# Diagonal prefix sums: the last block's fold, row sums and last 64 places placed differently over the engines

## The chip, the cores and the metric

The kernel runs on one core of one Trainium2 chip. The metric is the device time in microseconds of one execution. PE is the tensor engine (TensorE), DVE the vector engine (VectorE), ACT the scalar engine (ScalarE), POOL GpSimd, and SP the sync engine, which here only issues writes and one early load.

## The reference

```python
B, H, W = 4, 4224, 4224          # x: float32
ps = np.cumsum(np.cumsum(x, axis=1), axis=2)
diag = np.diagonal(ps, axis1=1, axis2=2)
return np.cumsum(diag, axis=1)   # (4, 4224)
```

Place i of the result is the sum, over all k up to i, of the sum of the k+1 by k+1 corner of x. An element in row r and column c therefore counts in place i with the weight i - max(r, c) + 1, where that is positive.

## The kernel before

Only elements on and below the diagonal band are needed row by row, and those right of it column by column, but together they are the whole of x: 285 MB are read. All loads but one are issued by POOL in float32 and land in SBUF as bf16. For each of the four batches the rows are taken in strips of 768 (tile `strip`, six rows on each of 128 partitions), and a last strip of 384. Three strip buffers let the loads run ahead of the work.

`add_up` handles a strip. TensorE adds the columns right of the strip's diagonal square into `d` (PSUM, 11 groups of 384 places), by matmuls whose stationary operand is one column of ones placed by `sel`. VectorE cuts the part above the diagonal out of the square (`mu`) and takes it out of the strip. ScalarE (`act_sum`, an ACTIVATE with an accumulator) and VectorE (`row_sums`) share the sums along the rows. At the end of a batch the row sums go into `d` too, and two scans along the places turn `d` into the results: `whole_sums` for batches 0 to 2, `last_sums` for batch 3.

The last batch ends in a stretch of its own, since nothing comes after it that could hide its work. Its last 384 rows (from `T0` on) are split. Their first 256 are part a (`part_a`, two halves of 128 rows), of which the columns of `head` were loaded at the very start. The last 128 rows are part b (`part_b`): four blocks of R = 32 rows, each spread over all 128 partitions as 32 rows by 4 pieces of 1024 columns, one load a block, with the last block cut into 768 and 256 columns. The diagonal square of part b is `diag_b`; it is loaded and summed (`dtot`) after strip 1 of the last batch.

The last 384 places are then gathered on one partition in three PSUM rows: `fin_a` (the first 256), `fin_b` (the last 128) and `fin_e` (what block 3 adds to the last 32). `weigh_a` and `weigh_b` are matmuls with a column of row sums as the stationary operand and a weight matrix streaming: `weights[p, i]` is i - p + 1 where positive, and `weights4` is the same for part b's blocks, where four partitions share a row. In order, as the code lists it: the fold of part a by `ident_h` into `fold_a`; block 0 by eight matmuls into `fold`, copied to `by` by ScalarE; `dtot`; the first row of `last_sums`; VectorE's `row_sums` of `fold_a` and their sum with the head's (`arows`); `by`; the four matmuls with `arows`; blocks 1 and 2, each summed half by ScalarE and half by VectorE (`pair_sum`, into `bsum`) and weighed into `fin_b`; block 3 in three pieces (`esum`), weighed into `fin_e`; and the sum of `fin_e` with the last 32 of `fin_b`, as `ye`.

The order is written by hand: the schedule is manual, so each engine runs its instructions in program order, and a wait holds up all that stands behind it on that engine. SP issues, in this order: the load of `head`; `yl`'s first 256 places; `whole_sums`; `last_sums`; `yl`'s next 96; `ye`, the last 32. POOL issues the loads. The lines that matter in the profile are L225 and L232 (all matmuls, by `matmul` and `matmul_on`), L267 (`act_sum`), L272 (`row_sums`), L282 (`pair_sum`), L498 (the scans), L533 (the copy to `by`), L540 (`arows`), L554 and L573 (`yl`), L579 (`ye`), and the writes L555, L558, L561, L574 and L580.

Of the kernel before, what the change touches and what calls it, by code (L numbers as in the profile page):

```python
# [8 lines left out]
FP32 = mybir.dt.float32  # L9
BF16 = mybir.dt.bfloat16  # L10
I32 = mybir.dt.int32
AX = mybir.AxisListType
# [5 lines left out]
def kernel(  # L18
# [14 lines left out]
    nc = tc.nc  # L33

    B, H, W = x.shape
    N = H
    P = 128
    F = 3
    F2 = 2 * F
    GW = P * F  # L40
# [3 lines left out]
    T0 = LG * GW  # L44
# [4 lines left out]
    consts = ctx.enter_context(tc.tile_pool(name="consts", bufs=1))  # L49
# [4 lines left out]
    last = ctx.enter_context(tc.tile_pool(name="last", bufs=1))  # L54
# [41 lines left out]
    hs = last.tile([P, 3], FP32, name="hs")  # L96
# [25 lines left out]
    for i in range(1, NBUF):  # L122
# [51 lines left out]
    def between_groups(name, turned):  # L174
# [35 lines left out]


    R = P // 4
    steps = consts.tile([P, P], I32, name="steps")
    nc.gpsimd.iota(steps, pattern=[[4, P]], base=7, channel_multiplier=-1)
    nc.vector.tensor_single_scalar(
        out=steps, in_=steps, scalar=2, op=ALU.arith_shift_right
    )
    weights4 = consts.tile([P, P], FP32, name="weights4")
    nc.vector.tensor_scalar_max(out=weights4, in0=steps, scalar1=0.0)

    ident_h = consts.tile([P, P], BF16, name="ident_h")
    nc.vector.tensor_copy(out=ident_h, in_=ident)
# [1 line left out]
    def matmul(o, lhsT, rhs, start=False):  # L224
        nc.tensor.matmul(  # L225
            o, lhsT=lhsT, rhs=rhs, start=start, stop=False, skip_group_check=True
        )

    def matmul_on(o, lhsT, rhs):

        te = nc.tensor
        te.add_instruction(  # L232
            mybir.InstMatmult(
                start_tensor_calc=False,
                stop_tensor_calc=False,
                tile_position=(0, 0),
                tile_size=(P, P if lhsT.shape[-1] > 64 else 32),
                bass_skip_group_check=True,
                ldweights=False,
                name=nc.get_next_instruction_name(),  # L240
                engine=te.engine,
                ins=[
                    te.lower_ap(rhs, opt=False),
                    te.lower_ap(lhsT, opt=False, for_matmul_weights=True),
                ],
                outs=[te.lower_ap(o)],
            )
        )

    weights4_h = consts.tile([P, P], BF16, name="weights4_h")  # L250
    nc.vector.tensor_copy(out=weights4_h, in_=weights4)
    ones_col = consts.tile([P, 1], FP32, name="ones_col")
    nc.vector.memset(ones_col, 1.0)

# [9 lines left out]
    def act_sum(acc, src):  # L264
        w = src.shape[-1]
        dump = dumpool.tile([P, 2176], BF16, name="dump")
        nc.scalar.activation(  # L267
            out=dump[:, :w], in_=src, func=ACT.Copy, accum_out=acc
        )

    def row_sums(acc, src):
        nc.vector.reduce_sum(out=acc, in_=src, axis=AX.X)  # L272
# [3 lines left out]
    def pair_sum(acc, src):  # L276

        w = src.shape[-1] // 2
        if not pairs:
            pairs.append(last.tile([P, 288], FP32, name="pair"))  # L280
        pair = pairs[0]
        nc.vector.scalar_tensor_tensor(  # L282
            out=pair[:, :w],
            in0=src[:, :w],
            scalar=1.0,
            in1=src[:, w:],
            op0=ALU.mult,
            op1=ALU.add,
            accum_out=acc,
        )  # L290
# [23 lines left out]
        nc.vector.memset(rows3[i], 0.0)  # L314


    asum = last.tile([P, 2, 2], FP32, name="asum")
    dtot = last.tile([P, 1], FP32, name="dtot")
    hu = last.tile([P, 3], FP32, name="hu")
    hmu = last.tile([P, 3, GW], BF16, name="hmu")  # L320
    for h in range(2):
        w = GW - h * P
        masked(hmu[:, h, :w], head[:, h, HC - w : HC], um1[:, :w], hu[:, h : h + 1])
    nc.vector.tensor_sub(out=asum[:, :, 0], in0=hs[:, 0:2], in1=hu[:, 0:2])

    whole_sums = last.tile([NG, LB, GW], FP32, name="whole_sums")
    last_sums = last.tile([NG, GW], FP32, name="last_sums")

    for b in range(B):
        whole = b < LB  # L330
# [8 lines left out]

        def row_of(j):  # L340
            return (j + t0) % NG

        def columns(j, lo, hi, rhs, same=False):
# [53 lines left out]
        for s in range(ns):  # L397
            strip = prefetched.pop(0) if prefetched else None
            if strip is None:
                strip = strip_tile()  # L400
                load_rows(strip, b, s * F2 * P)
            add_up(
                strip, F2, s * F2 * P, acc6[:, s], um6, by_rows=whole and s > 0
            )
            if not whole and s == 0:
                diag_b = last.tile([P, P], BF16, name="diag_b")
                nc.gpsimd.dma_start(out=diag_b, in_=x[b, TB:N, TB:N])
            if not whole and s == 1:
                row_sums(hs[:, 2:3], diag_b)
                masked(hmu[:, 2, :P], diag_b, um1[:, :P], hu[:, 2:3])  # L410
                nc.vector.tensor_sub(out=dtot, in0=hs[:, 2:3], in1=hu[:, 2:3])
                for h in range(3):
                    columns(LG, h * P, GW, hmu[:, h, : GW - h * P], h > 0)
        a6 = acc6[:, :ns]
        sum_up(a6)
        for h in range(2):
# [90 lines left out]
            continue  # L507


        M0 = 2 * P  # L510
        E0 = GW - R
        fin_a = psum_s.tile([1, M0], FP32, name="fin_a")
        fin_b = psum_s.tile([1, P], FP32, name="fin_b")
        fin_e = psum_s.tile([1, R], FP32, name="fin_e")
        yl = last.tile([1, GW], FP32, name="yl")
        ye = last.tile([1, R], FP32, name="ye")

        def weigh_a(rows, w, start=False):

            matmul(fin_a, rows, w[..., :M0], start=start)  # L520

        def weigh_b(rows, w, r0=0, start=False):

            matmul(fin_b[:, r0:], rows, w[..., : P - r0], start=start)


        c0, c1 = acuts[1]
        fold_in(fold_a, part_a, c0, c1, 256)
        by_ps = psum_s.tile([P, P], FP32, name="fold")
        for c in range(0, CB, P):  # L530
            matmul(by_ps, part_b[:, 0, c : c + P], weights4_h, start=c == 0)
        by = last.tile([P, P], FP32, name="by")
        nc.scalar.copy(out=by, in_=by_ps)  # L533
        weigh_b(dtot, weights, start=True)
        weigh_b(ones_col[0:1], last_sums[0:1, M0:])


        row_sums(asum[:, :, 1], fold_a)
        arows = last.tile([P, 2], FP32, name="arows")
        nc.vector.tensor_add(out=arows, in0=asum[:, :, 0], in1=asum[:, :, 1])  # L540
        weigh_b(ones_col, by)
        weigh_a(arows[:, 0:1], weights, start=True)
        matmul(fin_a[:, P:], arows[:, 1:2], weights[:, :P])
        weigh_b(arows[:, 0:1], weights[:, M0:])
        weigh_b(arows[:, 1:2], weights[:, P:])


        bsum = last.tile([P, 2, 2], FP32, name="bsum")
        esum = last.tile([P, 3], FP32, name="esum")
        act_sum(bsum[:, 0, 0:1], part_b[:, 1, :512])  # L550
        pair_sum(bsum[:, 0, 1:2], part_b[:, 1, 512:])
        for i in (1, 0):
            weigh_b(bsum[:, 0, i : i + 1], weights4, R)
        nc.vector.tensor_add(out=yl[:, :M0], in0=fin_a, in1=last_sums[0:1, :M0])  # L554
        nc.sync.dma_start(  # L555
            out=out[b, T0 : T0 + M0].unsqueeze(0), in_=yl[:, :M0]
        )
        nc.sync.dma_start(  # L558
            out=out[:LB, :].rearrange("b (g i) -> g b i", i=GW), in_=whole_sums
        )  # L560
# [2 lines left out]
        )  # L563
        act_sum(bsum[:, 1, 0:1], part_b[:, 2, :448])
        pair_sum(bsum[:, 1, 1:2], part_b[:, 2, 448:])
        for i in (1, 0):
            weigh_b(bsum[:, 1, i : i + 1], weights4, 2 * R)


        act_sum(esum[:, 0:1], part_b[:, 3, :320])  # L570
        pair_sum(esum[:, 1:2], part_b[:, 3, 320:bcut])
        pair_sum(esum[:, 2:3], part_b[:, 3, bcut:])
        nc.scalar.copy(out=yl[:, M0:], in_=fin_b)  # L573
        nc.sync.dma_start(  # L574
            out=out[b, T0 + M0 : T0 + E0].unsqueeze(0), in_=yl[:, M0:E0]
        )
        for k in (1, 0, 2):
            matmul(fin_e, esum[:, k : k + 1], weights4[:, :R], start=k == 1)
        nc.vector.tensor_add(out=ye, in0=fin_e, in1=yl[:, E0:])  # L579
        nc.sync.dma_start(out=out[b, T0 + E0 : N].unsqueeze(0), in_=ye)  # L580


# [28 lines left out]
```

## Time and profile before

| | |
|---|---|
| median of 10 runs | 667.34 us (667.16 to 667.73) |
| the profiled execution's own time | 667.34 us |
| its span, first to last instruction | 665.6 us |
| busy: PE / DVE / ACT / POOL | 205.9 / 380.9 / 136.1 / 31.7 us |
| DMA | 143.23 MB moved as written to SBUF and HBM, 215 GB/s mean; HBM read 285.47 MB |
| last load issued by POOL | 634.03 us |
| batch 2's last scan (`whole_sums` complete) | ends 521.33 us |
| batch 3's last scan (`last_sums` complete) | ends 659.78 us |
| SP's issue of `whole_sums` / `last_sums` / `ye` | 662.23 / 662.59 / 663.69 us |

All stamps count from the start of the span. A line of the timeline gives the start, the duration, the engine, the line of the code, the operation, and the tiles it writes and reads; in brackets stands the idle time of the engine before it and what ended that. A matmul in float32 is run as two passes, so "x4" of such matmuls are two. PEld is the load of a matmul's stationary operand. A line of the DMA view gives a queue (q0 POOL's, q1 SP's), its packets, its megabytes, and its share of the 16 DMA engines' time in the stretch.

### The profile page before, as it was taken

Reading aid. Unit: us, or ns where it says so; the run is one execution under the profiler, and the core shown is the slowest. Engines: PE = TensorE matmul, PEld = TensorE weight load, DVE = VectorE, ACT = ScalarE, POOL = GpSimd, SP = SyncE. Lnnn points to the kernel's source line nnn. Section 1 sums busy time; section 2 is a strip of 40 time slices with the busy share of each in tenths; the row PEclk is TensorE's granted clock in tenths of the full one; section 3 lists DMA queues with packets and bytes.
Section 4 is the critical chain, followed back from the end, with each engine's and each line's share of the span. In section 5 each row is a group of like instructions: output and inputs, shape, how many; then the busy total and the mean of one; then the engine's idle time right before and its main releaser. Section 6 shows DMA issues by size and latency. Waiting matters only on the chain.

```text
span 665.6 us, 2498 instructions
## 1 busy us (share of the span) xinstructions
PE 205.9 (31%) x948; PEld 93.8 (14%) x948; DVE 380.9 (57%) x176; ACT 136.1 (20%) x219; POOL 31.7 (5%) x60
## 2 busy tenths in 40 slices
PE   0071522302117143140311723404021354350428
PEld 0030211100003021010100311201000131120103
DVE  4161828476946173756794526456589433352866
ACT  0001120406300103040630020304063002030434
POOL 4300000000000000000000000000000000001000
PEclk9995857656559585665655857657565595775758
DMA  9999999999999999999999999999999999999998
GB/s 203 219 219 219 219 219 219 213 210 212 219 219 219 218 220 219 218 213 215 212 219 220 217 216 219 219 218 219 209 218 216 220 215 218 219 218 218 215 206 163
DMA packets 7666, 143.23 MB, mean 215 GB/s; under 512 B 698, under 2 KB 998, under 8 KB 2150
## 3 DMA queue, kind: packets, MB, share of 16 engines
q0 software_dynamic: 7312, 142.47, 100.0%
q1 hardware_dynamic: 342, 0.61, 0.4%
q8 instruction: 7, 0.11, 0.1%
q14 instruction: 5, 0.04, 0.0%
HBM read 285.47 MB, written 0.07 MB: 429 GB/s over the span
## 4 chain that ended last, share of the span: by engine, by line
DVE 50%; another core or an unknown queue 32%; DMA 14%; POOL 1%; issue 1%; PE 1%; DVEq 0%; POOLq 0%
DVE acc L272 26%; DMA strip<-in_x_dram 14%; DVE rowed L272 7%; DVE mu L367 7%; DVE strip L368 7%; PE d L225 1%; POOL um L107 1%; DVE um L106 1%; DMA head<-in_x_dram 1%; DVE c L498 0%; DVE whole_sums L498 0%; POOL strip L463 0%; DVE pu L272 0%; DVE whole_sums L293 0%
## 5 line engine op out<-in xcount | busy, mean ns | idle before, releaser
L267 ACT ACTIVATE dump<-strip 128x416 bf16<-128x416 bf16 (+6 forms) x108 | 124.4, 1152 | 520.3 <-DMA strip<-in_x_dram 517.6
L367 DVE TENSOR_TENSOR mu<-strip,um 128x4608 bf16<-128x4608 bf16 (+1 forms) x24 | 52.4, 2184 | 255.2 <-DMA strip<-in_x_dram 255.1
L272 DVE TENSOR_REDUCE acc<-strip 128x6 f32<-128x4608 bf16 (+6 forms) x23 | 195.9, 8519 | 0.4
L232 PEld LDWEIGHTS <-sel 128*11 128x11 bf16 x643 | 66.4, 103 | 477.2 <-issue 447.7
L225 PE MATMUL d<-strip,sel 128*11 128x384 bf16 x90 | 37.0, 411 | 281.9 <-DMA strip<-in_x_dram 281.9
L232 PE MATMUL d<-strip,sel 128*11 128x384 bf16 x441 | 116.3, 407 | 13.8 <-DMA strip<-in_x_dram 13.8
L368 DVE TENSOR_TENSOR strip<-strip,mu 128x4608 bf16<-128x4608 bf16 (+1 forms) x24 | 52.4, 2183 | 1.0
L225 PE MATMUL d<-mu,sel 128*11 128x384 bf16 x43 | 16.3, 379 | 108.4 <-DVE mu L367 108.4
L272 DVE TENSOR_REDUCE rowed<-strip 128x384 f32<-128x2304 bf16 x12 | 48.9, 4078 | 0.0
L232 PE MATMUL d<-mu,sel 128*11 128x384 bf16 x200 | 46.2, 365 | 0.0
L76 POOL DMA_DIRECT2D strip<-in_x_dram x23 | 15.6, 680 | 535.6 <-DVE acc L272 293.6
L267 ACT ACTIVATION_READ_ACCUMULATOR dump<-strip 128x1 f32 x108 | 20.1, 186 | 0.0
L225 PE MATMUL d<-rowed,sel_f 128*11 128x384 f32 x24 | 11.8, 580 | 21.0 <-DVE rowed L272 21.0
L225 PEld LDWEIGHTS <-sel 128*11 128x11 bf16 x134 | 13.6, 102 | 24.4 <-issue 12.5
L225 PE MATMUL d<-ident,rows 128*11 128x128 f32 x24 | 5.2, 378 | 16.8 <-DVE rows L428 16.8
L272 DVE TENSOR_REDUCE pu<-d 11x1 f32<-11x384 f32 x4 | 2.2, 545 | 6.2 <-PE d L225 6.2
L107 POOL TENSOR_SCALAR_AFFINE_SELECT um<-um 128x4608 bf16<-128x4608 bf16 (+1 forms) x2 | 5.2, 2621 | 8.6 <-DVE um L106 8.5
L106 DVE MEMSET um<- 128x4608 bf16 (+1 forms) x2 | 4.9, 2458 | 1.1 <-issue 1.1
L225 PE MATMUL d<-halves,rows 128*11 128x64 f32 x48 | 5.3, 288 | 0.0
L225 PEld LDWEIGHTS d<-ident,rows 128*11 128x11 f32 x24 | 2.5, 117 | 18.9 <-DVE rows L428 11.7
L225 PEld LDWEIGHTS d<-rowed,sel_f 128*11 128x11 f32 x24 | 1.4, 92 | 25.5 <-DVE rowed L272 25.2
L225 PEld LDWEIGHTS d<-halves,rows 128*11 128x11 f32 x48 | 4.8, 128 | 1.3 <-issue 1.1
(106 smaller groups left out, 62.0 us busy)
## 6 DMA issues: line engine op xcount, KB each, us to landing
strip<-in_x_dram POOLq DMA_DIRECT2D x18, 6336.0 KB, 72.7
strip<-in_x_dram POOLq DMA_DIRECT2D x7, 3168.0 KB, 55.8
strip<-in_x_dram POOLq DMA_DIRECT2D x1, 1080.0 KB, 49.9
strip<-in_x_dram POOLq DMA_DIRECT2D x1, 768.0 KB, 52.8
strip<-in_x_dram POOLq DMA_DIRECT2D x3, 256.0 KB, 54.1
head<-in_x_dram SPq DMA_DIRECT2D x1, 528.0 KB, 3.7
strip<-in_x_dram POOLq DMA_DIRECT2D x1, 192.0 KB, 43.2
strip<-in_x_dram POOLq DMA_DIRECT2D x1, 64.0 KB, 28.6
```

The lines of the kernel that those rows point to most:

```text
L76: nc.gpsimd.dma_start(out=o, in_=x[b, r0 : r0 + f * P, :].rearrange("(p f) w -> p f w", f=f))
L106: nc.vector.memset(um, 1.0)
L107: nc.gpsimd.affine_select(out=um, in_=um, compare_op=ALU.is_gt, fill=0.0, base=0, pattern=[[-1, f], [1, f * P]], channel_multiplier=-f,)
L225: nc.tensor.matmul(o, lhsT=lhsT, rhs=rhs, start=start, stop=False, skip_group_check=True)
L232: te.add_instruction(mybir.InstMatmult(start_tensor_calc=False, stop_tensor_calc=False, tile_position=(0, 0), tile_size=(P, P if lhsT.shap ...
L267: nc.scalar.activation(out=dump[:, :w], in_=src, func=ACT.Copy, accum_out=acc)
L272: nc.vector.reduce_sum(out=acc, in_=src, axis=AX.X)
L367: nc.vector.tensor_mul(out=mu, in0=block, in1=um)
L368: nc.vector.tensor_sub(out=block, in0=block, in1=mu)
```

## The change

The change touches the last stretch and what it needs. ScalarE sums `fold_a` by two ACTIVATEs into `asum`, in place of VectorE's `row_sums`; the head's row sums (`ahead`) are no longer added to them, but weighed by matmuls of their own, together with `dtot`, right after strip 1 of the last batch. `fin_a`, `fin_b` and `fin_e` are allocated at the start of that batch for it.

The last 64 places (S = 64, 32 before) go to 64 partitions: `fin_e` becomes 64 by 129. Its last column takes the last 64 of `yl`, turned onto partitions by a one-row matmul, and block 2's weighed sums; its other 128 columns take block 3, which is no longer summed first: TensorE streams it in eight pieces of 128 columns, with `weights4_hw`, the bf16 weights widened by 32 columns, as the stationary operand. VectorE sums the 129 columns into `ye`, 64 partitions of one value, and `ye` is written from there. The copy of `fin_b` into `yl` moves from ScalarE to VectorE and ahead of block 2's weighing; `yl` is written once, as 320 places, after `whole_sums` and `last_sums`.

```diff
-    steps = consts.tile([P, P], I32, name="steps")
-    nc.gpsimd.iota(steps, pattern=[[4, P]], base=7, channel_multiplier=-1)
+    steps = consts.tile([P, R + P], I32, name="steps")
+    nc.gpsimd.iota(steps, pattern=[[4, R + P]], base=7 - 4 * R, channel_multiplier=-1)
...
-    weights4 = consts.tile([P, P], FP32, name="weights4")
-    nc.vector.tensor_scalar_max(out=weights4, in0=steps, scalar1=0.0)
+    weights4_w = consts.tile([P, R + P], FP32, name="weights4_w")
+    nc.vector.tensor_scalar_max(out=weights4_w, in0=steps, scalar1=0.0)
+    weights4 = weights4_w[:, R:]
...
-    weights4_h = consts.tile([P, P], BF16, name="weights4_h")
-    nc.vector.tensor_copy(out=weights4_h, in_=weights4)
+    weights4_hw = consts.tile([P, R + P], BF16, name="weights4_hw")
+    nc.vector.tensor_copy(out=weights4_hw, in_=weights4_w)
+    weights4_h = weights4_hw[:, R:]
...
-    nc.vector.tensor_sub(out=asum[:, :, 0], in0=hs[:, 0:2], in1=hu[:, 0:2])
+    nc.vector.tensor_sub(out=ahead, in0=hs[:, 0:2], in1=hu[:, 0:2])
...
+    M0 = 2 * P
+    S = 2 * R
+    E0 = GW - S
...
+        if not whole:
+            fin_a = psum_s.tile([1, M0], FP32, name="fin_a")
+            fin_b = psum_s.tile([1, P], FP32, name="fin_b")
+            fin_e = psum_s.tile([S, P + 1], FP32, name="fin_e")
...
+        def weigh_rows(rows, start=False):
+
+            matmul(fin_a, rows[:, 0:1], weights[:, :M0], start=start)
+            matmul(fin_a[:, P:], rows[:, 1:2], weights[:, :P])
+            weigh_b(rows[:, 0:1], weights[:, M0:])
+            weigh_b(rows[:, 1:2], weights[:, P:])
...
                     columns(LG, h * P, GW, hmu[:, h, : GW - h * P], h > 0)
+                weigh_b(dtot, weights, start=True)
+                weigh_rows(ahead, start=True)
...
+        for h in range(2):
+            act_sum(asum[:, h : h + 1], fold_a[:, h])
         by = last.tile([P, P], FP32, name="by")
         nc.scalar.copy(out=by, in_=by_ps)
-        weigh_b(dtot, weights, start=True)
         weigh_b(ones_col[0:1], last_sums[0:1, M0:])
-
-
-        row_sums(asum[:, :, 1], fold_a)
-        arows = last.tile([P, 2], FP32, name="arows")
-        nc.vector.tensor_add(out=arows, in0=asum[:, :, 0], in1=asum[:, :, 1])
+        weigh_rows(asum)
         weigh_b(ones_col, by)
-        weigh_a(arows[:, 0:1], weights, start=True)
-        matmul(fin_a[:, P:], arows[:, 1:2], weights[:, :P])
-        weigh_b(arows[:, 0:1], weights[:, M0:])
-        weigh_b(arows[:, 1:2], weights[:, P:])
...
         nc.vector.tensor_add(out=yl[:, :M0], in0=fin_a, in1=last_sums[0:1, :M0])
         nc.sync.dma_start(
-            out=out[b, T0 : T0 + M0].unsqueeze(0), in_=yl[:, :M0]
-        )
-        nc.sync.dma_start(
             out=out[:LB, :].rearrange("b (g i) -> g b i", i=GW), in_=whole_sums
         )
...
         pair_sum(bsum[:, 1, 1:2], part_b[:, 2, 448:])
+        nc.vector.tensor_copy(out=yl[:, M0:], in_=fin_b)
+        nc.sync.dma_start(
+            out=out[b, T0 : T0 + E0].unsqueeze(0), in_=yl[:, :E0]
+        )
+
+
+        matmul(fin_e[:, P:], yl[:, E0:], ones_col[0:1], start=True)
         for i in (1, 0):
-            weigh_b(bsum[:, 1, i : i + 1], weights4, 2 * R)
-
-
-        act_sum(esum[:, 0:1], part_b[:, 3, :320])
-        pair_sum(esum[:, 1:2], part_b[:, 3, 320:bcut])
-        pair_sum(esum[:, 2:3], part_b[:, 3, bcut:])
-        nc.scalar.copy(out=yl[:, M0:], in_=fin_b)
-        nc.sync.dma_start(
-            out=out[b, T0 + M0 : T0 + E0].unsqueeze(0), in_=yl[:, M0:E0]
-        )
-        for k in (1, 0, 2):
-            matmul(fin_e, esum[:, k : k + 1], weights4[:, :R], start=k == 1)
-        nc.vector.tensor_add(out=ye, in0=fin_e, in1=yl[:, E0:])
-        nc.sync.dma_start(out=out[b, T0 + E0 : N].unsqueeze(0), in_=ye)
+            matmul(fin_e[:, P:], weights4[:, :S], bsum[:, 1, i : i + 1])
+        for c in range(0, CB, P):
+            piece = part_b[:, 3, c : c + P]
+            if c == 0:
+                matmul(fin_e[:, :P], weights4_hw[:, :S], piece, start=True)
+            else:
+                matmul_on(fin_e[:, :P], weights4_hw[:, :S], piece)
+        nc.vector.reduce_sum(out=ye, in_=fin_e, axis=AX.X)
+        nc.sync.dma_start(out=out[b, T0 + E0 : N].unsqueeze(1), in_=ye)
```

`matmul_on` is `matmul` without a new start of its accumulation; it takes a tile size of 64 columns besides 32 and 128. On SP, `whole_sums` is now the first issue after the load of `head`, and waits for VectorE's scan alone.

More of the change, by code (lines that the diff above doesn't have):

```diff
@@ L236, in matmul_on @@
                 tile_position=(0, 0),
-                tile_size=(P, P if lhsT.shape[-1] > 64 else 32),
+                tile_size=(P, P if lhsT.shape[-1] > 64 else 64 if lhsT.shape[-1] > 32 else 32),
                 bass_skip_group_check=True,
@@ L314 @@
         nc.vector.memset(rows3[i], 0.0)
-    asum = last.tile([P, 2, 2], FP32, name="asum")
+    ahead = last.tile([P, 2], FP32, name="ahead")
+    asum = last.tile([P, 2], FP32, name="asum")
     dtot = last.tile([P, 1], FP32, name="dtot")
@@ L341, in row_of, with weigh_b @@
             return (j + t0) % NG
+        if not whole:
+            fin_a = psum_s.tile([1, M0], FP32, name="fin_a")
+            fin_b = psum_s.tile([1, P], FP32, name="fin_b")
+            fin_e = psum_s.tile([S, P + 1], FP32, name="fin_e")
+        def weigh_b(rows, w, r0=0, start=False):
+            matmul(fin_b[:, r0:], rows, w[..., : P - r0], start=start)
+        def weigh_rows(rows, start=False):
[3 more added lines that the diff above has]
+            weigh_b(rows[:, 1:2], weights[:, P:])
         def columns(j, lo, hi, rhs, same=False):
@@ L507 @@
             continue
[L510 to L514, printed above, removed]
-        yl = last.tile([1, GW], FP32, name="yl")
[L516 to L524, printed above, removed]
+        yl = last.tile([1, GW], FP32, name="yl")
+        ye = last.tile([S, 1], FP32, name="ye")
         c0, c1 = acuts[1]
@@ L531 @@
             matmul(by_ps, part_b[:, 0, c : c + P], weights4_h, start=c == 0)
+        for h in range(2):
+            act_sum(asum[:, h : h + 1], fold_a[:, h])
         by = last.tile([P, P], FP32, name="by")
         nc.scalar.copy(out=by, in_=by_ps)
-        weigh_b(dtot, weights, start=True)
         weigh_b(ones_col[0:1], last_sums[0:1, M0:])
-        row_sums(asum[:, :, 1], fold_a)
-        arows = last.tile([P, 2], FP32, name="arows")
-        nc.vector.tensor_add(out=arows, in0=asum[:, :, 0], in1=asum[:, :, 1])
+        weigh_rows(asum)
         weigh_b(ones_col, by)
-        weigh_a(arows[:, 0:1], weights, start=True)
-        matmul(fin_a[:, P:], arows[:, 1:2], weights[:, :P])
-        weigh_b(arows[:, 0:1], weights[:, M0:])
-        weigh_b(arows[:, 1:2], weights[:, P:])
         bsum = last.tile([P, 2, 2], FP32, name="bsum")
-        esum = last.tile([P, 3], FP32, name="esum")
         act_sum(bsum[:, 0, 0:1], part_b[:, 1, :512])
```

## The prediction

> **What bounds the kernel now.** I read the page's 40 slices first, then the chain of waits, then the timeline of the last 8 us, and last the DMA view of the same stretch.
>
> ```profile
> span 665.6 us, 2498 instructions
> DMA  9999999999999999999999999999999999999998
> GB/s 203 219 219 219 219 219 219 213 210 212 219 219 219 218 220 219 218 213 215 212 219 220 217 216 219 219 218 219 209 218 216 220 215 218 219 218 218 215 206 163
> q1 hardware_dynamic: 342, 0.61, 0.4%
> ```
>
> The DMA engines are full from the first slice to the last but one, at about 219 GB/s; no compute engine passes 57%. Up to about 661 us only what lengthens the stream of loads costs time. After it, the tail counts: what stands between the last landings and the last write. From the timeline:
>
> ```profile
> 659.71 0.65 DVE L272 TENSOR_REDUCE asum<-fold_a 128x2 f32<-128x512 f32 x1
> 659.83 0.08 PEld L225 LDWEIGHTS fin_b<-last_sums,ones_col 1*1 1x1 f32 x2 [0.32 <-DVE last_sums L498]
> 660.14 0.09 PEld L225 LDWEIGHTS fin_b<-by,ones_col 128*1 128x1 f32 x2 [0.22 <-issue]
> 660.61 0.81 PE L225 MATMUL fin_a<-weights,arows 128*1 128x256 f32 x4
> 661.43 0.58 ACT L267 ACTIVATE dump<-strip 128x448 bf16<-128x448 bf16 x1 [0.51 <-DMA strip<-in_x_dram]
> 662.36 0.39 DVE L282 SCALAR_TENSOR_TENSOR pair<-strip 128x224 f32<-128x224 bf16 x1
> 662.80 0.29 DVE L282 SCALAR_TENSOR_TENSOR pair<-strip 128x128 f32<-128x128 bf16 x1
> 662.82 0.55 PE L225 MATMUL fin_e<-weights,esum 128*1 128x32 f32 x6
> 662.82 0.24 ACT L573 COPY yl<-fin_b 1x128 f32<-1x128 f32 x1
> 663.48 0.18 DVE L579 TENSOR_TENSOR ye<-fin_e,yl 1x32 f32<-1x32 f32 x1 [0.38 <-PE fin_e L225]
> 663.69 0.23 SPq L580 DMA_DIRECT2D out_dram<-ye  x1
> ```
>
> The last piece of block 3 lands at 634.03 + 28.6 = 662.63 us (its issue, and the page's time to landing of the 64 KB load). Then VectorE's pair sums, three small matmuls, one add, and ye's write at 663.69, which takes 665.6 - 663.69 = 1.91 us to the end of the span. From landing to issue there are only 1.06 us.
>
> **What the Trainium skill says.** "TensorE: Matmul & The Clock Gate", Back-to-back issue gap: about 56 ns from start to start at 128 columns with a warm clock. The trace agrees: eight 128-column matmuls for block 0 took 0.61 us, each 219 ns long, so (0.61 - 0.22)/7 = 56 ns; the granted clock is 1.00 from 656 us on. The same page, LDWEIGHTS: a load takes its columns divided by 1.2 ns, 53 ns for 64; no row here has a 64-column load. "DMA: Bandwidth & Descriptors", Why a DMA increments its semaphore by 16 and not by 1: a write is spread over the largest number up to 16 that divides its slowest dimension, and each of those engines adds a semaphore write. The trace agrees: whole_sums 33 rows + 11, last_sums 10 + 10, three one-row writes 3 + 3 make 70, and the last 107 us show
>
> ```profile
> q1 hardware_dynamic: 70, 0.07, 0.4%
> ```
>
> Same page, Specifications: transfers under 512 B are read-modify-written. Two of the three one-row writes are that short already, and no run yet shows a price for it; 4-byte rows are nowhere in this trace.
>
> **The change part by part.**
>
> *Constants and early weighing.* The iota grows from 128 to 160 columns (0.24 us now, so +0.06), three VectorE operations with it, near 23 us, under loads in flight: 0. Ten float32 passes (two per float32 matmul) for dtot and the head's row sums move to after strip 1 of the last batch. They wait for dtot at 572.08 us; behind them TensorE has nothing until strip 2 lands at 588.98. Column slope from the rows at 32, 64, 96, 128 and 256 columns (190, 218, 246, 273, 378 ns): 0.83 ns a column a pass, 0.17 us at the end. 8 x 128 + 2 x 256 columns make 1.3 us, twice that at half clock, against 16.9 us free: 0. In the tail the dtot pair (0.21 us) goes, but TensorE then waits for the scan ending at 659.78 anyway: 0.
>
> *Writes.* SP's first tail write, behind which whole_sums and last_sums stood, is gone. whole_sums now waits only for batch 2's scan, done at 521.3 us, so it leaves inside the full stream, where before it left at 662.23 into empty engines. Its price, from the DMA view of 662.9 to 663.3 us:
>
> ```profile
> q1 hardware_dynamic: 18, 0.03, 47.1%
> ```
>
> 0.471 x 16 x 0.4 / 18 = 0.17 us a row. 33 rows are 5.5 us of engine time: 0.34 over 16 engines, 0.50 on each of the 11 that take three rows. By bytes, 50.7 KB at 219 GB/s, it is 0.23. It may be nothing, if the engines that finish last are among the five left free. I take **+0.3** (0 to 0.5). last_sums now leaves at about 659.85, one row on ten engines: up to 0.17 on the last landings, which have slack below: 0 (0 to 0.17).
>
> *The fold on ScalarE.* fold_a is complete at 657.81 + 1.24 = 659.05. VectorE's 0.65 us sum and 0.16 us add (rows ready at 660.56) give way to two 256-wide ACTIVATEs. From 471, 577 and 629 ns at 320, 448 and 512 columns a 256-wide one takes 0.42, with its accumulator read a period of 0.53: ready at 659.64 and 660.17. Behind them ScalarE's `by` copy slips from 659.80 to 660.45 (its end), block 1's part from 660.20 to 660.48, ready 661.21; block 2 lands at 661.40 and is not late.
>
> *TensorE's order.* last_sums' pair at 659.84; the next may start at 660.14 (as `by` does now, 0.22 us of "issue" after the one-row matmul). asum's four matmuls 0.43 + 0.21 + 0.43 (as arows' now), to 661.21; `by` 0.21; block 1's two 0.32: streamed by 661.74, ended 661.91. VectorE then copies fin_b, after its block 2 pair sum (661.93): 0.15 + 128 x 1.03 ns = 0.28 (slope from the 32- and 256-wide adds, 0.18 and 0.41), so 661.99 to 662.27. This is the added wait: TensorE is in order, and behind the yl matmul stand block 2's two and all eight of block 3; nothing of block 3 can stream before. SP's single yl write (two before) follows the copy too, at 662.30, with only ye behind it. From 662.33: six passes with 64 float32 columns of weights. Nothing here shows such a load; carry's tiny passes run at 0.05, the skill's 53 ns is the bf16 figure, I take 0.08, and 0.1 for leaving the one-row shape: 0.58, to 662.91 (bounds 662.63 and 663.3). Block 3: seven starts at 56 ns and 0.22: **663.52**, all pieces long landed. VectorE's 64 x 129 sum follows at 663.61 and takes 0.15 + 129 x 1.03 ns = 0.29 (from 653 ns at 512), ends 663.90; ye issues at about 663.93, **+0.24** on 663.69. If TensorE stood ready at the last landing, it would be two matmuls (0.28), hand-over 0.1 and 0.29 after 662.63: 663.33, **-0.36**. Upper bound, block 3's weight loads not hidden (107 ns a step): +0.6.
>
> *The last write.* 64 rows of 4 B on 16 engines, instead of one of 128 B. SP's issue takes 0.23 now, 0.33 for last_sums' ten rows, 0.44 for the head's 256; one packet of ye takes about 10 ns (0.7% of 16 engines over 0.1 us), so four in a row hardly count; sixteen receipts instead of one. I take **+0.25** (0 to +1.5: the bound above stands for writes to the same few hundred bytes that get in each other's way, which no row prices).
>
> Sum: 0.3 + 0.24 + 0.25 = **+0.8 us**. The profiled execution took 667.34, its span 665.6 and 1.74 around it; it equals the median, 667.34. So 668.1.
>
> **The rivals.** *Block 3 keeps pace with the loads.* TensorE waits for the landing, not for yl: -0.36, whole_sums hidden or not, write +0.25: about 667.2, unmeasurable. For it: PE is ahead of the landings before. Against: every pass up to yl is back to back from 660.14.
>
> *Slower: the 4-byte write.* One mechanism, at ye's write: the 64 writes of 4 B, each below 512 B, are merged one after another at the memory, and nothing follows to hide it. At 10 ns each (ye's one packet now) that is 0.6 us, at 167 ns (a row of whole_sums) 10.7; I take 30 ns, near the low end as 4 B are far from 1536: +1.9 us, with the 0.54 above about 669.8. It decides from a write of 1.91 + 0.8 = 2.7 us on. For it: 256 bytes written by 16 engines. Against: ye's one packet is short, and the 1.91 us are mostly a fixed return trip.
>
> *Not doing what it says.* The compiled order has a weight load ahead of each of block 3's matmuls, so the weights aren't held; it matters only if loads don't hide (the +0.6 above).
>
> **How the numbers follow.** 0.2% is 1.33 us, about what a measurement of this kernel can tell from no change. Forecast 0.60 (0.54 within, 0.06 slower); keeping pace 0.18 (0.15 within, 0.03 faster, which would need a shorter load stream, since the tail can't give 1.33 us); the slow write 0.22 (0.18 slower, 0.04 within). Range: low end 0 - 0.36 + 0 = 667.0; high end 0.5 + 0.6 + 1.1, with half of the slow write's cases: 669.5.
>
> **What would show it.** Right: whole_sums issued near 521 us, not at 662; the yl copy ending near 662.3, and block 3's first matmul after it, not at a landing; ye issued at 663.9; from ye's issue to the end 2.1 to 2.3 us. Wrong: block 3 waiting on a DMA; landings in the last 20 us unshifted; the last write over 2.7 us; or a span below 665.

## The result, and the profile after

The changed kernel takes 673.23 us (median of 8 runs, 672.74 to 674.35) against 667.31 us (29 runs, 667.08 to 668.33): 0.9% longer, ratio 1.0090 with a 95% interval of 1.0081 to 1.0098. The forecast was 668.1 us, and the range ended at 669.5.

The profiled execution has a span of 671.5 us, 5.9 more than before. First the page: the head line, and the DMA and GB/s rows of the 40 slices.

```profile
span 671.5 us, 2516 instructions
DMA  9999999999999999999999999999999999999994
GB/s 201 217 217 217 218 217 217 217 217 217 217 219 217 218 217 217 216 216 217 217 217 218 217 217 217 217 217 217 217 217 217 219 217 216 216 217 217 215 205 87
```

The DMA row shows the stream of loads as full as it was. In the GB/s row 217 stands where mostly 219 stood, the dips to 209 to 213 of before are gone, and block 2 of the last rows lands only 0.42 us later, as shown below; a slice is 16.8 us here and was 16.6. What differs is the last slice: 87 GB/s in place of 163. More of it is empty. The timeline of the tail:

```profile
659.56 0.38 ACT L269 ACTIVATE dump<-fold_a 128x256 bf16<-128x256 f32 x1 [5.51 <-PE fold_a L233]
660.07 0.38 ACT L269 ACTIVATE dump<-fold_a 128x256 bf16<-128x256 f32 x1
660.17 0.08 PEld L226 LDWEIGHTS fin_b<-last_sums,ones_col 1*1 1x1 f32 x2 [0.43 <-DVE last_sums L523]
661.85 0.58 ACT L269 ACTIVATE dump<-strip 128x448 bf16<-128x448 bf16 x1 [0.51 <-DMA strip<-in_x_dram]
662.31 0.28 DVE L565 COPY yl<-fin_b 1x128 f32<-1x128 f32 x1
662.64 0.19 PEld L226 LDWEIGHTS fin_e<-ones_col,yl 1*64 1x64 f32 x2 [0.61 <-DVE yl L565]
663.07 0.11 PEld L226 LDWEIGHTS <-weights_hw 128*64 128x64 bf16 x1
663.15 0.55 PE L233 MATMUL fin_e<-strip,weights_hw 128*64 128x128 bf16 x7
663.74 0.28 DVE L580 TENSOR_REDUCE ye<-fin_e 64x1 f32<-64x129 f32 x1 [1.16 <-PE fin_e L233]
664.05 0.54 SPq L581 DMA_DIRECT2D out_dram<-ye  x1
```

Block 2's landing (it releases the ACTIVATE at 661.85, 661.43 before) comes 0.42 us later, and ye issues at 664.05, 0.36 later than before. From the landing to the issue it is 2.20 us where it was 2.26. So the engines' work has not become slower. The rest of the span is 671.5 - 664.05 = **7.45 us** for ye's write, which took 1.91. That is 5.54 of the 5.9 us. SP's list of waits for these last microseconds has the wait itself (us in all, times, longest), before and then after, and the DMA view of 664.05 to 671.5 us, in 40 slices of 0.19 us, has the packets of the kernel after:

```profile
SPq L606 <- DMA out_dram<-ye: 0.2, 1, 0.2
```

```profile
SPq L607 <- DMA out_dram<-ye: 5.5, 1, 5.5
```

```profile
DMA  0000001000000000000000000000000000000000
...
DMA packets 80, 0.00 MB, mean 0 GB/s; under 512 B 80, under 2 KB 80, under 8 KB 80
...
q1 hardware_dynamic: 80, 0.00, 0.5%
...
out_dram<-ye SPq DMA_DIRECT2D x1, 0.2 KB, 6.5
```

Only the seventh slice, from 665.17 us, has a digit other than 0. All 80 packets (64 rows and 16 semaphore writes) have been through the engines by 665.6 us, in 0.5% of 16 x 7.45 us = 0.6 us of engine time. The last line is the issue with its time to landing. After the packets no engine of any kind shows work for nearly 5 us, until the write is reported landed at 664.05 + 6.5 = 670.55. So the time passes after the last packet that the profile shows; where it passes, no view says.

### The profile page after: what moved, and what is told of

The parts are those of the page before. It is cut to its first block, busy times and chain, and to the rows that moved or that the text cites. A ratio compares the mean times of both kernels' runs of the same rounds, so it can differ in the third digit from the quotient of the medians.

```text
span 671.5 us, 2516 instructions
## 1 busy us (share of the span) xinstructions
PE 208.6 (31%) x960; PEld 95.6 (14%) x960; DVE 380.1 (57%) x171; ACT 136.2 (20%) x220; POOL 31.7 (5%) x60
## 4 chain that ended last, share of the span: by engine, by line
DVE 53%; another core or an unknown queue 34%; DMA 8%; PE 3%; issue 1%; POOL 1%; DVEq 0%
DVE acc L274 27%; DVE mu L390 7%; DMA strip<-in_x_dram 7%; DVE strip L391 7%; DVE rowed L274 7%; PE d L226 1%; DMA head<-in_x_dram 1%; DVE c L523 1%; POOL um L107 1%; DVE um L106 1%; DVE whole_sums L523 0%; PE fold L233 0%; DVE pu L274 0%; PE d L233 0%
## 5 line engine op out<-in xcount | busy, mean ns | idle before, releaser
L226 PE MATMUL d<-strip,sel 128*11 128x384 bf16 x90 | 37.5, 417 | 279.9 <-DMA strip<-in_x_dram 279.9
L233 PE MATMUL d<-strip,sel 128*11 128x384 bf16 x441 | 117.6, 411 | 13.8 <-DMA strip<-in_x_dram 13.8
L226 PE MATMUL d<-ident,rows 128*11 128x128 f32 x24 | 5.2, 379 | 16.8 <-DVE rows L453 16.8
```

What stands on the lines that cost most here:

```text
L226: nc.tensor.matmul(o, lhsT=lhsT, rhs=rhs, start=start, stop=False, skip_group_check=True)
L233: te.add_instruction(mybir.InstMatmult(start_tensor_calc=False, stop_tensor_calc=False, tile_position=(0, 0), tile_size=(P, P if lhsT.shap ...
```

## The experiments

The time from ye's issue to the end of the span is called the write's time below. It is read from one profile each, the span less the issue's stamp; the landings of the loads move by some tenths of a microsecond between executions, and by more at times, so differences in spans alone are not used for it. The kernels whose names begin with w leave a part of the result unwritten or put it elsewhere; they ran once each.

**What in the last write costs.** Four kernels: the layout alone put into the kernel before, and three that move or thin out the rows in the changed kernel.

```diff
 # b_rows32, from the kernel before
-        fin_e = psum_s.tile([1, R], FP32, name="fin_e")
+        fin_e = psum_s.tile([R, 1], FP32, name="fin_e")
...
-        ye = last.tile([1, R], FP32, name="ye")
+        ye = last.tile([R, 1], FP32, name="ye")
...
-            matmul(fin_e, esum[:, k : k + 1], weights4[:, :R], start=k == 1)
-        nc.vector.tensor_add(out=ye, in0=fin_e, in1=yl[:, E0:])
-        nc.sync.dma_start(out=out[b, T0 + E0 : N].unsqueeze(0), in_=ye)
+            matmul(fin_e, weights4[:, :R], esum[:, k : k + 1], start=k == 1)
+        matmul(fin_e, yl[:, E0:], ones_col[0:1])
+        nc.vector.tensor_copy(out=ye, in_=fin_e)
+        nc.sync.dma_start(out=out[b, T0 + E0 : N].unsqueeze(1), in_=ye)
 # w61_one_engine, from the changed kernel, as all that follow with ye
-        nc.sync.dma_start(out=out[b, T0 + E0 : N].unsqueeze(1), in_=ye)
+        nc.sync.dma_start(out=out[b, T0 + E0 : N - 3].unsqueeze(1), in_=ye[:61])
 # w64_apart (the first lines in all kernels that use the room of whole_sums)
-        nc.sync.dma_start(
-            out=out[:LB, :].rearrange("b (g i) -> g b i", i=GW), in_=whole_sums
-        )
...
-        nc.sync.dma_start(out=out[b, T0 + E0 : N].unsqueeze(1), in_=ye)
+        flat = out[:LB, :].rearrange("b n -> (b n)")[: S * 198]
+        nc.sync.dma_start(out=flat.rearrange("(p k) -> p k", k=198)[:, 0:1], in_=ye)
 # w64_wide64
-        ye = last.tile([S, 1], FP32, name="ye")
+        ye = last.tile([S, 16], FP32, name="ye")
...
+        flat = out[:LB, :].rearrange("b n -> (b n)")[: S * 16]
+        nc.sync.dma_start(out=flat.rearrange("(p k) -> p k", k=16), in_=ye)
```

b_rows32:

> The kernel before with nothing changed but the layout of its last 32 places: they lie on 32 partitions, and ye is written as 32 rows of 4 B. The time from ye's issue to the end is 1.91 us before and 7.45 us in the changed kernel (64 rows). Same place: writes to the same few hundred bytes are done one after another at the memory, (7.45 - 1.91)/64 = 0.087 us each, so 32 rows give 1.91 + 2.8 = 4.7 us and about 670 us in all. Fixed: any 4-byte row makes the write's return long, whatever their number, so 7.4 us and about 673. Engine: each DMA engine does its own rows one after another, 5.54/4 = 1.4 us each, two rows on each of 16 engines: 4.7 us too.

w61_one_engine:

> The changed kernel, with only 61 of ye's 64 rows written (the last three places are left out). 61 is prime, so one DMA engine takes all rows, in place of 16 with four each. Same place: 61 writes to the same 256 bytes, 1.91 + 61 x 0.087 = 7.2 us from ye's issue to the end, whoever sends them. Engine: 61 x 1.4 us, over 80 us. Fixed: 7.4 us. Sixteen returns (the number of engines and semaphores is what costs): about 2.5 us.

w64_apart:

> The changed kernel, with ye's 64 rows of 4 B written 792 B apart, into the room of whole_sums, which is not written. Same place: no two rows meet, so 2.2 to 2.6 us from ye's issue to the end. Engine or fixed: 7.4 us as now. The landings of the last loads come about 0.35 us earlier than in the changed kernel if whole_sums' write inside the stream is what delayed them.

w64_wide64:

> The changed kernel, with ye's 64 rows widened to 64 B each, side by side over 4 KB in the room of whole_sums, which is not written; ye's value is the first of each row. Same place, if a place is 64 B or less: 2.2 to 2.6 us from ye's issue to the end. Same place, if a place is 512 B: eight rows meet, 1.91 + 8 x 0.087 = 2.6 to 3. Fixed for any row under 512 B, or engine: 7.4 us.

b_rows32 measured 669.54 us, ratio 1.0037 (1.0023 to 1.0051), and a write of 668.4 - 664.24 = 4.16 us. So the layout of the last places is enough to make the kernel before slower, with nothing else of the change in it. Its issue and wait:

```profile
664.24 0.32 SPq L581 DMA_DIRECT2D out_dram<-ye  x1
```

```profile
SPq L607 <- DMA out_dram<-ye: 2.3, 1, 2.3
```

w61_one_engine: 672.5 - 663.59 = 8.9 us. It sends 62 packets (61 and one semaphore write), so one engine carries them all, and the write is no shorter than with sixteen. w64_apart: 666.4 - 663.82 = 2.58 us. w64_wide64: 666.2 - 663.56 = 2.64 us. SP's wait in w64_apart, and then w61_one_engine's packets from 664 us on and its wait:

```profile
SPq L605 <- DMA out_dram<-ye: 0.8, 1, 0.8
```

```profile
DMA packets 62, 0.00 MB, mean 0 GB/s; under 512 B 62, under 2 KB 62, under 8 KB 62
```

```profile
SPq L607 <- DMA out_dram<-ye: 7.4, 1, 7.4
```

The same 64 rows of 4 B on the same sixteen engines cost 0.8 us of waiting when they lie apart, and 5.5 when they lie side by side. "Fixed", "engine" and "sixteen returns" are out: a row of 4 B isn't slow by itself, one engine with 61 rows took nothing like 80 us, and with a single return the write was not short. Where the rows lie is what counts.

**What the rest of the change costs.** Four kernels, timed against the kernel before.

```diff
 # turned, from the changed kernel
-        nc.sync.dma_start(out=out[b, T0 + E0 : N].unsqueeze(1), in_=ye)
+        ye_ps = psum_s.tile([1, S], FP32, name="fold")
+        matmul(ye_ps, ye, ident[:S, :S], start=True)
+        ye_row = last.tile([1, S], FP32, name="ye_row")
+        nc.vector.tensor_copy(out=ye_row, in_=ye_ps)
+        nc.sync.dma_start(out=out[b, T0 + E0 : N].unsqueeze(0), in_=ye_row)
 # turned_late: turned, with the two writes moved
+        nc.sync.dma_start(out=out[b, T0 : T0 + E0].unsqueeze(0), in_=yl[:, :E0])
         nc.sync.dma_start(out=out[:LB, :].rearrange("b (g i) -> g b i", i=GW), in_=whole_sums)
         nc.sync.dma_start(out=out[b, :T0].rearrange("(g i) -> g i", i=GW), in_=last_sums[1:NG])
-        nc.sync.dma_start(out=out[b, T0 : T0 + E0].unsqueeze(0), in_=yl[:, :E0])
 # b_whole, from the kernel before
+        nc.sync.dma_start(out=out[:LB, :].rearrange("b (g i) -> g b i", i=GW), in_=whole_sums)
         nc.sync.dma_start(out=out[b, T0 : T0 + M0].unsqueeze(0), in_=yl[:, :M0])
-        nc.sync.dma_start(out=out[:LB, :].rearrange("b (g i) -> g b i", i=GW), in_=whole_sums)
 # b_part1, from the kernel before
+                weigh_b(dtot, weights, start=True)      # after strip 1
+                weigh_rows(ahead, start=True)
...
+        for h in range(2):
+            act_sum(asum[:, h : h + 1], fold_a[:, h])
...
-        row_sums(asum[:, :, 1], fold_a)
...
+        weigh_rows(asum)
```

turned:

> The changed kernel, with ye's 64 values turned onto one partition by a matmul with the identity and copied, then written as one row of 256 B. If the 4-byte rows are the whole loss but some tenths, this takes off 5.5 us and pays about 0.5 for the matmul, the copy and two hand-overs: 668.2 us, and 1.9 us from ye's issue to the end. If something else of the change costs over a microsecond, it stays above 669.3.

b_whole:

> The kernel before, with whole_sums' write moved ahead of SP's first tail write, so that it leaves near 521 us inside the stream of loads, and nothing else. In the stream: 33 rows at 0.17 us spread over the engines delay all later landings by 0.3 us, 667.6 us, whereas profiles of one execution differ by that much in their landings and can't tell. Absorbed (the engines that finish last carry none of it): no change, within 0.1 us.

b_part1:

> The kernel before with the first part of the change alone: ScalarE sums the fold, the head's row sums and dtot are weighed after strip 1 of the last batch; writes and block 3 as before. Covered: no change (within 0.1 us), since ye still waits for the last landing, VectorE's pair sum, TensorE and VectorE. ScalarE late: its two sums push block 1's and block 2's sums back, and the end by up to 0.5 us.

turned_late:

> As turned, with the writes of whole_sums and last_sums behind yl's, so that both leave after the loads. If whole_sums in the stream costs 0.3 us, this is 0.3 under turned: 667.9 us. If it is absorbed, both are equal. If the late writes now stand in the way of ye's issue (SP takes about 0.35 us for each), ye waits at SP until about 663.6, earlier than it is ready, so no loss.

Beside 667.59 us for the kernel before (51 runs): turned 668.27, ratio 1.0013 (1.0005 to 1.0020); b_whole 667.90, 1.0005 (0.9997 to 1.0013); b_part1 667.37, 0.9999 (0.9990 to 1.0008); turned_late 668.20, 1.0005 (0.9997 to 1.0013). The ratios take in every run and are not the quotients of the medians. The timeline of turned shows what the turning costs and what it brings:

```profile
664.23 0.28 DVE L580 TENSOR_REDUCE ye<-fin_e 64x1 f32<-64x129 f32 x1 [1.16 <-PE fin_e L233]
664.56 0.27 PE L226 MATMUL fold<-ident,ye 64*1 64x64 f32 x2 [0.38 <-DVE ye L580]
664.87 0.21 DVE L584 COPY ye_row<-fold 1x64 f32<-1x64 f32 x1 [0.36 <-PE fold L226]
665.11 0.23 SPq L585 DMA_DIRECT2D out_dram<-ye_row  x1
```

From the end of VectorE's sum (664.51) to the issue it is 0.60 us, where the changed kernel has 0.03; the write then takes 667.1 - 665.11 = 2.0 us. For 0.57 us of turning, about 5.4 us of writing go: the medians say 673.23 - 668.27 = 5.0. So the whole change with its last write turned costs about 0.13% (0.9 us), of which the turning itself is 0.57. b_part1 shows no change, as covered work should. The times can't settle the whole_sums term: the interval of b_whole holds both no change and the 0.3 us, and turned and turned_late overlap. The landings say more. Twenty kernels of this record have a profile. In seven of them whole_sums leaves inside the stream, and there ScalarE starts on block 2 at 661.44 to 663.82 us, median 661.64; in the thirteen others it starts at 661.39 to 663.89, median 661.49. w64_apart, without the write, starts 0.44 us before the changed kernel, as was expected if the write is to blame, but w16_rows (described below) has the write and starts as early:

```profile
521.25 0.37 SPq L557 DMA_DIRECT2D out_dram<-whole_sums  x1
```

```profile
661.46 0.58 ACT L269 ACTIVATE dump<-strip 128x448 bf16<-128x448 bf16 x1 [0.46 <-DMA strip<-in_x_dram]
```

So most of the changed kernel's 0.42 us is the scatter of one execution, and what the write costs, if anything, is less than the scatter.

**What counts as one place.** By the first four kernels 64 rows that meet cost (7.45 - 2.58)/64 = 0.076 us each. Four kernels vary the distance, the number and the width of the rows.

```diff
 # w64_at64: k=16;  w64_at16: k=4
+        flat = out[:LB, :].rearrange("b n -> (b n)")[: S * 16]
+        nc.sync.dma_start(out=flat.rearrange("(p k) -> p k", k=16)[:, 0:1], in_=ye)
 # w16_rows
+        nc.sync.dma_start(out=out[b, T0 + E0 : N - 48].unsqueeze(1), in_=ye[:16])
 # w64_wide32: as w64_wide64, with 8 columns in place of 16
```

w64_at64:

> The changed kernel, with ye's 64 rows of 4 B written 64 B apart over 4 KB, in the room of whole_sums, which is not written. At 792 B apart the write took 2.58 us from issue to end, side by side 7.45: 0.076 us for each of the 64. If writes meet only within 64 B: 2.6 us. Within 256 B, four meet: 2.9. Within 512 B, eight meet: 3.2. If they meet however near they are within 4 KB: 7.4.

w64_at16:

> The same, 16 B apart over 1 KB. Four meet in 64 B: 2.9 us from ye's issue to the end. Sixteen meet in 256 B: 3.8. Thirty-two meet in 512 B: 5.0. All in 1 KB: 7.4.

w16_rows:

> The changed kernel, with only the first 16 of ye's 64 rows written, side by side in 64 B, one on each of 16 engines (48 places are left out). In proportion to the rows that meet: 2.58 + 16 x 0.076 = 3.8 us from ye's issue to the end. If the cost were the engines' own (four rows each now): it falls to a quarter too; if it were the return of any 4-byte row: 7.4. With 32 rows 4.16 and 64 rows 7.45 this is the third point of a line.

w64_wide32:

> The changed kernel, with ye's rows widened to 32 B each, side by side over 2 KB in the room of whole_sums, which is not written. 64 B rows side by side took 2.64 us. If what meets is two partial writes of one 64 B piece: 2.7 us. If partial writes meet within 256 B: eight of them, 3.2. If 32 B is a whole unit: 2.6.

The writes took 666.3 - 663.67 = 2.63 us (64 B apart), 666.4 - 663.80 = 2.60 (16 B apart), 666.1 - 663.89 = 2.21 (16 rows) and 667.0 - 664.44 = 2.56 (32 B wide). SP's waits, w64_at16 and then w16_rows:

```profile
SPq L605 <- DMA out_dram<-ye: 0.8, 1, 0.8
```

```profile
SPq L607 <- DMA out_dram<-ye: 0.5, 1, 0.5
```

The five kernels with 64 rows and at most sixteen of them in one 256 B agree within 0.1 us (2.56 to 2.64), which shows how far one profile can be trusted here. By the 0.076 us the second and third should have been 3.8 if sixteen rows meet in 256 B. I took that for a refutation of "same place", and put in its stead that rows of one engine within 16 B of each other wait for each other. Four kernels on that:

```diff
 # four_by16
+        for q in range(0, S, 16):
+            nc.sync.dma_start(
+                out=out[b, T0 + E0 + q : T0 + E0 + q + 16].unsqueeze(1), in_=ye[q : q + 16]
+            )
 # four_stepped
+        for j in range(4):
+            nc.sync.dma_start(
+                out=out[b, T0 + E0 : N].rearrange("(i j) -> i j", j=4)[:, j : j + 1], in_=ye[j : S : 4]
+            )
 # w64_at8: as w64_at64, with k=2
 # w61_at16: as w64_at16, with [:61, 0:1] and ye[:61]
```

four_by16:

> The changed kernel, with ye written by four DMAs of 16 rows, each side by side in 64 B and with one row on each engine. Neighbours of one engine: no engine has two rows within 16 B, so the last DMA, issued some 3 x 0.32 us after the first, takes 2.2 us: 3.2 us from the first issue to the end, about 669 us in all. An engine coming back within 256 B: three waits of 1.6 us, 7 us or more, about 673.

four_stepped:

> As four_by16, but each of the four DMAs takes every fourth place, so that an engine's four rows are neighbours within 16 B, one in each DMA. Neighbours of one engine: the waits come back, less the 0.32 us between the issues: 6 to 7.5 us from the first issue to the end, about 672 in all. If engines don't keep to the same rows from one DMA to the next, or if the wait arises only within one DMA: 3.2 us, as four_by16.

w64_at8:

> The changed kernel, with ye's 64 rows written 8 B apart over 512 B in the room of whole_sums, which is not written. At 16 B apart it took 2.60 us from issue to end, at 4 B 7.45. Neighbours within 16 B of one engine: two rows meet, one wait of 1.6 us, 4.2 us. If only rows that touch each other meet: 2.6. Back within 256 B: two of an engine's four rows in each 256 B or more, 4.2 or above.

w61_at16:

> The changed kernel, with 61 of ye's rows on one engine (the last three are left out), 16 B apart in the room of whole_sums, which is not written. Side by side they took 8.9 us from issue to end. Neighbours: the three waits of 1.6 us (4.9 in all, all groups of four at once) go, what is left is the price of 61 rows on one engine: about 4.0 us. If the time is that of 61 rows on one engine, however they lie: 8.9.

four_by16 took 674.57 us in all (ratio 1.0104, 1.0087 to 1.0121) and 672.8 - 663.90 = 8.9 us from the first issue, four_stepped 673.73 us (1.0088, 1.0073 to 1.0103) and 671.7 - 663.59 = 8.1. The theory of neighbours gave 3.2 for the first, so it falls: an engine's rows lay 64 B apart there, and it was as slow as any. w64_at8 took 669.0 - 664.54 = 4.46 us, w61_at16 666.6 - 663.95 = 2.65; SP's waits in this order:

```profile
SPq L605 <- DMA out_dram<-ye: 2.6, 1, 2.6
```

```profile
SPq L605 <- DMA out_dram<-ye: 1.1, 1, 1.1
```

w61_at16 shows that 61 rows on one engine are cheap too once they lie apart: 2.65 us against 8.9 side by side. It also rules out the other reading put down for four_by16, an engine that comes back to the same 256 B: its one engine does so up to fifteen times in each.

What fits the kernels that write from sixteen engines by one DMA is the first idea with another line: 32 rows in one 256 B took 4.16 (b_rows32) and 4.46 us (w64_at8), 64 rows 7.45, so about 0.1 us a row on a start of about 0.9, and at sixteen rows that line (2.5 us) has only just reached what the write takes in any case. It was drawn after these times were known, and it gives less than four_by16 (8.9) and four_stepped (8.1) took; why four DMAs are slower than one stays open. The last two kernels test it: they keep 64 rows side by side and only move where a multiple of 256 B cuts them.

```diff
 # w64_off128: o = 32;  w64_off64: o = 16 (elements)
+        nc.sync.dma_start(out=out[:LB, :].rearrange("b n -> (b n)")[o : o + S].unsqueeze(1), in_=ye)
```

w64_off128:

> The changed kernel, with ye's 64 rows of 4 B side by side as now, but starting 128 B after a multiple of 256 B, in the room of whole_sums, which is not written: 32 rows lie on each side of a boundary. Aligned 256 B: 0.87 + 32 x 0.103 = 4.2 us from issue to end, some tenths more for SP's longer issue. Density alone, or larger places: 7.4 us as in the changed kernel, where all 64 lie in one aligned 256 B.

w64_off64:

> The same, starting 64 B after a multiple of 256 B: 48 rows before the boundary and 16 after it. Aligned 256 B: 0.87 + 48 x 0.103 = 5.8 us. Density alone, or larger places: 7.4. Places of 128 B: 32 rows at most in one, 4.2.

They took 668.7 - 664.16 = 4.54 us and 670.3 - 664.13 = 6.17 us. SP's waits, w64_off128, then w64_off64:

```profile
SPq L604 <- DMA out_dram<-ye: 2.7, 1, 2.7
```

```profile
SPq L604 <- DMA out_dram<-ye: 4.4, 1, 4.4
```

The same 64 rows, the same engines, the same packets, side by side each time: 7.45, 6.17 and 4.54 us with at most 64, 48 and 32 of them in one aligned 256 B. How densely the rows lie can't do that, since it is the same in all three. Places of 128 B can't either: the fullest would hold 32 rows in all three. Nor can places of 512 B: there w64_at16 would have 32 rows in one and take about 4.5 us, and it took 2.60. (This takes it that the output begins at a multiple of 256 B, which the order of the three times bears out; the changed kernel's rows begin 67,328 = 263 x 256 bytes into it, and so fill one place.) All kernels with one write, by the number of rows in the fullest 256 B:

| rows in one 256 B | kernels | write's time, us |
|---|---|---|
| 1 to 8 | w64_apart, w64_at64, w64_wide64, w64_wide32 | 2.56 to 2.64 |
| 16 | w16_rows; w64_at16, w61_at16 | 2.21; 2.60, 2.65 |
| 32 | b_rows32; w64_at8, w64_off128 | 4.16; 4.46, 4.54 |
| 48 | w64_off64 | 6.17 |
| 64 | changed kernel | 7.45 |
| 61, one engine | w61_one_engine | 8.9 |

SP's issue is a part of these times: 0.53 to 0.54 us with 64 rows, 0.32 with 16 or 32, 0.23 with 61 on one engine. Among those with 64 rows it is (7.45 - 4.5)/32 = 0.09 us a row from 32 rows on, and (7.45 - 2.60)/48 = 0.10 from sixteen on. Up to sixteen, nothing is seen. That small writes to one aligned 256 B complete one after another is the reading of these times. That this happens at the memory and at no stage before it is argued, not shown: the engines' packets are over by 665.6 us, and no view here reaches behind them. Why one engine is slower than sixteen (8.9 us against 0.9 + 61 x 0.1 = 7.0 by the line) stays open.

## Why the prediction was wrong

**The step that failed is the last write's term, +0.25 us with a bound of +1.5.** It measured +5.54. I priced what the profile of before could show: SP's longer issue (0.54 us, 0.44 at most expected), short packets (right: 80 of them in 0.6 us of engine time), sixteen returns in place of one. These make the 2.6 us of rows that lie apart, 0.7 over before: more than the 0.25, and inside the bound. The other 4.9 us come from 64 rows in one aligned 256 B, which the term named in its bound and gave no price. The bound of 1.5 had no line of a profile behind it, and the range ended where it ended because of it.

**The slower rival named the mechanism, as far as the runs reach, and mis-sized it.** It said that the writes are merged one after another at the memory, and decided from a write of 2.7 us on; the write took 7.45. The runs show a time that grows with each row, as of writes done one after another, but only beyond sixteen rows in one 256 B; that rows are merged, or at the memory, they don't show. Its working bracketed a row between 10 ns and 167 ns, and then took 30 ns, because 4 B are far from 1536. Measured is about 0.09, in the middle of that bracket; with it the rival gives 0.54 + 64 x 0.09 = 6.3 us more, close to the 5.9 measured. The size of a row was no reason to go to the low end: the bracket's ends are packets' times on the engines, and the wait begins after the packets. Its chance, 0.22, was too small for the same cause, and the range ended at 669.5, below this rival's own 669.8.

**The short rows.** The Trainium skill, "DMA: Bandwidth & Descriptors", Specifications, says that rows below 512 B are treated differently; it doesn't say what that costs. No run here writes a row of 512 B or more in ye's place, so that cost isn't measured. Among the short rows the runs show what matters: 64 rows of 4, 32 or 64 B all take 2.6 us with at most sixteen of them in one 256 B, and 7.45 with all of them in one. The same page's count of engines, under Why a DMA increments its semaphore by 16 and not by 1, held: 64 + 16 packets, and 61 + 1 for the prime number of rows.

**The added wait: right in kind, wrong in price.** I expected block 3 to stand behind the yl copy, and ye to issue at 663.93, 0.24 late. It issued at 664.05, but that nearness is luck: a later landing made up for two terms that were too large. The yl matmul does wait for the copy (0.61 us idle, above), and block 3 starts only at 663.07. But measured from block 2's landing ye is issued 0.06 us earlier than before. The two terms: the copy started 0.10 us sooner relative to that landing than in my count (662.31 - 0.42 = 661.89, not 661.99), and the six passes with 64-column float32 weights took 662.64 to 663.07 = 0.43 us, not 0.58. Block 3's eight steps came out as worked out, 663.09 + 7 x 0.056 + 0.22 = 663.70, and so, but for 0.01, did the 0.28 us of VectorE's sum. The weight loads that the compiled order has ahead of block 3's matmuls are hidden: from 663.15 its steps are (0.55 - 0.22)/6 = 55 ns. The rival in which block 3 keeps pace with the loads didn't happen.

**Writes in the stream: +0.3, not settled, probably too much.** whole_sums was issued at 521.3 us as expected. The landing of block 2 is 0.42 us later in that profile, but strip 1's (559.1 us, well after 521.3) is not, and the medians over the profiles with and without the write are 0.15 us apart, in a scatter of over 2 us. b_whole's interval, -0.03% to +0.13%, holds 0 and the 0.3 us.

**Covered parts.** The early weighing, the constants and the fold on ScalarE were costed at nothing. b_part1 has the first and the last of these, and its ratio of 0.9999 (0.9990 to 1.0008) agrees; the wider constants were not run alone. ScalarE's sums were ready at 660.03 and 660.54, some tenths late with the landings, and block 2 wasn't held up.

No kernel that writes the whole result beats the kernel before by a difference that can be measured. turned, the nearest use of the new tail, is 0.13% slower; b_part1 is equal.

## What to carry to other kernels

A transposed result that is written straight from its partitions, one value a row, can cost more than the work it saves: count how many rows fall into one aligned 256 B of the destination, and from some sixteen on add about 0.1 us for each further one, as measured here with rows of 4 B from SP's queue. If the write is the last thing a kernel does, all of that is on the path; turning the values onto one partition cost 0.6 us here and saved 5.4. And where an operation has no line in the profile and the bracket spans a factor of ten or more, do not go to its low end without a reason, and let the range reach its other end.

## What was not expected of the hardware

Sixteen rows of 4 B in one 64 B, from sixteen engines, are as quick as rows hundreds of bytes apart (2.21 us with sixteen rows; 64 rows 792 B apart 2.58), while four times as many in 256 B take 7.45. During the wait no engine and no DMA queue shows anything: the profile's only trace of it is SP's idle time before the end, 5.5 us in place of 0.2, and a time to landing of 6.5 us for 256 bytes (1.7 us in w64_apart, with as many packets).
